# The weight and work tiles of an encoder kernel move to the top end of each SBUF partition

## The chip, the cores and the metric

The program runs on one core of one Trainium2 chip. The metric is the device time of one execution in microseconds (us); the matmul engine is called PE here, VectorE DVE, ScalarE ACT, GpSimd POOL. Before the change the median of three runs is 1266.83 us.

## The reference

A bidirectional encoder of four layers on 256 tokens with 1024 features, all in float32. Each layer is a token mixer and then a gated feed-forward block, both behind an RMS norm and with a residual add. The mixers are a gated short convolution (layers 0 and 3), attention in a neighbourhood (layer 1) and a Hyena long convolution (layer 2).

```python
for i in range(DEPTH):
    h = rmsnorm(x, norm_mix_g[i])
    y = short_conv_mixer(...) | neighborhood_attention(...) | hyena_mixer(...)
    x = x + y
    x = x + swiglu(rmsnorm(x, norm_ffn_g[i]), f_w13[i], f_w2[i])   # (silu(g) * u) @ w2, 2816 wide
```

## The kernel before, in words

Every weight passes through once. `wload` (lines 97 to 113) fetches a piece of 128 x 1024 floats by DMA into a tile `st`, has ACT round it into `hi` (float32r, line 107), and has DVE or POOL put the rest, `st - hi`, into `lo` (line 110). `st` has 5 buffers, `hi` and `lo` 6 each; all of them have 4096 bytes in a partition. Activations are split in the same way, so each product is three matmuls: high by high, low by high, high by low.

There are two kinds of matmul. In one the activations are the stationary operand (128 columns) and the weights stream past as the moving operand, 512 columns wide: `matmul3`, lines 127 to 131. It serves the first feed-forward product (tiles `pg`; 4 layers x 528 = 2112 matmuls, stationary tiles `xs`), the second (`accw`; 4 x 264 = 1056, stationary tiles `hid`), and the out-projections of the mixers (`accao`, `accbo`, `accco`; 192, 96 and 96, stationary tiles `mid`). In the other the weights are stationary and 256 columns of activations move: `mm3`, lines 115 to 120, for the in-projections of the short convolutions (`ai`, 1152) and of the Hyena mixer (`ci`, 576). The attention's in-projection (`bi`, 576, lines 549 to 551) has stationary activations and 256 moving columns of weights. Some small products of the long convolution's filters use the same forms (`ff`, `fh`).

The order of the work is the order in which the code is written, with small tables of lags (lines 41 to 50) for what is put between the matmuls; the change touches none of it. Between the pieces of the first feed-forward product stand four transposes each (`pth`, line 329), and in layers 0 and 1 the filters' small products.

SBUF tiles come from pools. A pool takes its room when it is opened, next to the pool opened before it, and gives it back when it is closed. Five pools stay open all the time (lines 58 to 62): `const`, `xsp` (tiles `xs`), `wst` (`st`), `wsp` (`hi`, `lo`) and `tp` (work tiles). The pools of a stage, such as those with `hid`, `mid` and the filters' tiles, are opened on top of them and closed with the stage.

Of the kernel before, what the change touches and what calls it, by code (L numbers as in the profile page):

```python
# [53 lines left out]
def encoder(ctx: ExitStack, tc: tile.TileContext, A: dict, out: bass.AP):  # L54
    nc = tc.nc
    ve, ac, pe, gp, sy = nc.vector, nc.scalar, nc.tensor, nc.gpsimd, nc.sync

    const = ctx.enter_context(tc.tile_pool(name="const", bufs=1))
    xsp = ctx.enter_context(tc.tile_pool(name="xsp", bufs=8))
    wst = ctx.enter_context(tc.tile_pool(name="wst", bufs=5))  # L60
    wsp = ctx.enter_context(tc.tile_pool(name="wsp", bufs=6))
    tp = ctx.enter_context(tc.tile_pool(name="tp", bufs=8))
    pp = ctx.enter_context(tc.tile_pool(name="pp", bufs=8, space=PSUM))
    dram = ctx.enter_context(tc.tile_pool(name="dram", bufs=1, space=DRAM))

# [922 lines left out]
```

## Time and profile before

| | us |
|---|---|
| median of 3 runs (1265.57 to 1267.26) | 1266.83 |
| the profiled execution's own time | 1265.59 |
| its span in the profile | 1263.7 |
| PE busy | 1217.6 (96%) |
| PE weight loads busy, beside the matmuls | 1055.2 (84%) |
| DVE busy | 841.5 (67%) |
| ACT busy | 636.2 (50%) |
| POOL busy | 272.9 (22%) |

[...] The rate is read from the starts: the time between the first and the last start of an unbroken row of matmuls, by the number of steps. The mean granted clock of PE is 0.99 of full speed, and the DMA queues move 182 GB/s on average.

### The profile page before, as it was taken

Reading aid. Unit: us, or ns where it says so; the run is one execution under the profiler, and the core shown is the slowest. Engines: PE = TensorE matmul, PEld = TensorE weight load, DVE = VectorE, ACT = ScalarE, POOL = GpSimd, SP = SyncE. Lnnn points to the kernel's source line nnn. Section 1 sums busy time; section 2 is a strip of 40 time slices with the busy share of each in tenths; the row PEclk is TensorE's granted clock in tenths of the full one; section 3 lists DMA queues with packets and bytes.
Section 4 is the critical chain, followed back from the end, with each engine's and each line's share of the span. In section 5 each row is a group of like instructions: output and inputs, shape, how many; then the busy total and the mean of one; then the engine's idle time right before and its main releaser. Section 6 shows DMA issues by size and latency. Waiting matters only on the chain.

```text
span 1263.7 us, 17703 instructions
## 1 busy us (share of the span) xinstructions
PE 1217.6 (96%) x6748; PEld 1055.2 (84%) x6748; DVE 841.5 (67%) x1023; ACT 636.2 (50%) x963; POOL 272.9 (22%) x228
## 2 busy tenths in 40 slices
PE   7999999999998999999988888999999999999998
PEld 7997888788998888887878887888888998888887
DVE  6867676786676647757678997655554776655542
ACT  6545554445576655543464444644443554544431
POOL 0111122333354212223226775000000000000000
PEclk9999999999999999999999999999999999999999
DMA  8656656565665565675754434556654655656661
GB/s 312 218 182 228 180 179 196 156 221 186 193 193 180 150 191 176 197 215 165 225 184 123 128 102 149 184 183 185 188 190 153 205 184 162 204 184 185 185 191 52
DMA packets 66892, 229.51 MB, mean 182 GB/s; under 512 B 9654, under 2 KB 10040, under 8 KB 66552
## 3 DMA queue, kind: packets, MB, share of 16 engines
q1 hardware_dynamic: 59824, 212.73, 53.9%
q0 software_dynamic: 4656, 9.73, 2.6%
q10 hardware_dynamic: 2328, 5.93, 1.4%
q8 instruction: 53, 0.87, 0.3%
q14 instruction: 31, 0.25, 0.1%
HBM read 222.04 MB, written 6.29 MB: 181 GB/s over the span
## 4 chain that ended last, share of the span: by engine, by line
PE 84%; DVE 9%; issue 2%; POOL 2%; ACT 2%; DMA 2%; ACTq 0%; SPq 0%; DVEq 0%; POOLq 0%
PE pg L129 13%; PE pg L131 13%; PE pg L130 13%; PE accw L129 6%; PE accw L131 6%; PE accw L130 6%; PE pth L329 2%; PE ai1a L118 1%; PE ai0a L119 1%; PE ai1a L119 1%; PE ai1a L120 1%; DMA bm<-in_rpb 1%; PE ai0a L120 1%; PE ai0a L118 1%; PE accao L131 1%
## 5 line engine op out<-in xcount | busy, mean ns | idle before, releaser
L76 DVE TENSOR_TENSOR low<-stw,hiw 128x1024 fp32r<-128x1024 f32 x246 | 304.8, 1243 | 225.9 <-ACT hiw L107 224.3
L107 ACT CAST hiw<-stw 128x1024 fp32r<-128x1024 f32 x268 | 280.7, 1052 | 298.6 <-PE pg L130 142.2
L129 PE MATMUL pg<-hiw,xsf 128*128 128x512 f32 x704 | 278.5, 397 | 0.5 <-ACT xsf L146 0.5
L131 PE MATMUL pg<-low,xsf 128*128 128x512 f32 x704 | 275.0, 391 | 0.0
L130 PE MATMUL pg<-hiw,xsf 128*128 128x512 f32 x704 | 274.3, 390 | 0.0
L131 PEld LDWEIGHTS pg<-low,xsf 128*128 128x128 f32 x704 | 132.4, 188 | 28.5
L129 PEld LDWEIGHTS pg<-hiw,xsf 128*128 128x128 f32 x704 | 132.4, 188 | 28.3 <-ACT xsf L146 1.9
L130 PEld LDWEIGHTS pg<-hiw,xsf 128*128 128x128 f32 x704 | 132.7, 188 | 26.6 <-DVE xsf L147 0.2
L129 PE MATMUL accw<-hiw,hid 128*128 128x512 f32 x352 | 139.7, 397 | 0.0
L131 PE MATMUL accw<-low,hid 128*128 128x512 f32 x352 | 138.5, 393 | 0.0
L130 PE MATMUL accw<-hiw,hid 128*128 128x512 f32 x352 | 138.0, 392 | 0.0
L76 POOL TENSOR_TENSOR low<-stw,hiw 128x1024 fp32r<-128x1024 f32 x22 | 54.4, 2474 | 171.4 <-ACT hiw L107 157.0
L131 PEld LDWEIGHTS accw<-low,hid 128*128 128x128 f32 x352 | 66.0, 188 | 15.9
L130 PEld LDWEIGHTS accw<-hiw,hid 128*128 128x128 f32 x352 | 66.2, 188 | 14.6
L129 PEld LDWEIGHTS accw<-hiw,hid 128*128 128x128 f32 x352 | 66.3, 188 | 14.0
L107 ACT CAST hiai<-stai 128x1024 fp32r<-128x1024 f32 (+1 forms) x49 | 48.8, 1013 | 38.4 <-PE ai1a L119 8.1
L76 DVE TENSOR_TENSOR loai<-stai,hiai 128x1024 fp32r<-128x1024 f32 (+1 forms) x49 | 56.9, 1178 | 15.7 <-ACT hiai L107 15.4
L320 ACT ACTIVATE sg<-pg,rtf 128x256 f32<-128x256 f32 x88 | 41.0, 468 | 45.2 <-PE pg L131 45.0
L321 DVE SCALAR_TENSOR_TENSOR hh<-pg,rtf,sg 128x256 f32<-128x256 f32 x88 | 41.8, 480 | 26.0 <-ACT sg L320 25.9
L118 PE MATMUL ci<-xsm,hici 128*128 128x256 f32 x192 | 56.6, 297 | 0.0
L551 PE MATMUL bi<-lobi,xsm 128*128 128x256 f32 x192 | 54.3, 283 | 2.0 <-DVE lobi L76 2.0
L550 PE MATMUL bi<-hibi,xsm 128*128 128x256 f32 x192 | 54.3, 283 | 1.7 <-DVE xsm L147 1.7
(243 smaller groups left out, 2478.0 us busy)
## 6 DMA issues: line engine op xcount, KB each, us to landing
stw<-in_f_w SPq DMA_DIRECT2D x264, 512.0 KB, 3.7
stai<-in_a_w_in SPq DMA_DIRECT2D x45, 512.0 KB, 4.3
stbi<-in_b_w_qkv SPq DMA_DIRECT2D x24, 512.0 KB, 4.2
stci<-in_c_w_in SPq DMA_DIRECT2D x24, 512.0 KB, 3.9
stao<-in_a_w_out SPq DMA_DIRECT2D x16, 512.0 KB, 3.7
hf<-ht POOLq DMA_DIRECT2D x16, 256.0 KB, 3.6
stbo<-in_b_w_out SPq DMA_DIRECT2D x8, 512.0 KB, 4.5
hq<-hf ACTq DMA_DIRECT2D x8, 512.0 KB, 3.6
```

The costliest lines, as they stand in the source:

```text
L76: (eng or ve).tensor_tensor(out=out_, in0=a, in1=b, op=op)
L107: ac.copy(out=hi[:, c], in_=st[:, c])
L118: pe.matmul(ps, hi[:, ws], xh, start=first, stop=False, **kw)
L119: pe.matmul(ps, hi[:, ws], xl, start=False, stop=False, **kw)
L120: pe.matmul(ps, lo[:, ws], xh, start=False, stop=last, **kw)
L129: pe.matmul(ps, xh, hi, start=first, stop=False, skip_group_check=True)
L130: pe.matmul(ps, xl, hi, start=False, stop=False, skip_group_check=True)
L131: pe.matmul(ps, xh, lo, start=False, stop=last, skip_group_check=True)
L320: ac.activation(sg, ps[h][:, :T], AF.Silu, scale=r)
L321: ve.scalar_tensor_tensor(out=hh[:, h * T : (h + 1) * T], in0=ps[h][:, T:], scalar=r, in1=sg, op0=ALU.mult, op1=ALU.mult)
L550: pe.matmul(o_, xl, hi[:, c], start=False, stop=False, skip_group_check=True)
L551: pe.matmul(o_, xh, lo[:, c], start=False, stop=k == KT - 1, skip_group_check=True)
```

## The change

Four of the five lasting pools are opened with `side="right"`: their tiles are packed from the top end of the partition down, and the pools of the stages, with `xsp`, from the bottom end up.

```diff
-    const = ctx.enter_context(tc.tile_pool(name="const", bufs=1))
+
+    wsp = ctx.enter_context(tc.tile_pool(name="wsp", bufs=6, side="right"))
+    wst = ctx.enter_context(tc.tile_pool(name="wst", bufs=5, side="right"))
+    tp = ctx.enter_context(tc.tile_pool(name="tp", bufs=8, side="right"))
+    const = ctx.enter_context(tc.tile_pool(name="const", bufs=1, side="right"))
     xsp = ctx.enter_context(tc.tile_pool(name="xsp", bufs=8))
-    wst = ctx.enter_context(tc.tile_pool(name="wst", bufs=5))
-    wsp = ctx.enter_context(tc.tile_pool(name="wsp", bufs=6))
-    tp = ctx.enter_context(tc.tile_pool(name="tp", bufs=8))
```

Both programs have the same instructions on every engine, in the same order and with the same waits; source lines from 58 on have a number higher by one. What differs are addresses. The table gives the first byte of each group of tiles in its partition, and that byte's remainder by 1024. All tiles of a group are whole multiples of 1024 bytes apart, and the operands inside them begin at steps of 512 bytes, so the remainder by 512 is that of every operand of the group.

| tiles | first byte before | remainder | first byte after | remainder |
|---|---|---|---|---|
| `xs` | 26624 | 0 | 16512 | 128 |
| `st` | 43008 | 0 | 159712 | 992 |
| `hi` | 63488 | 0 | 180192 | 992 |
| `lo` | 88064 | 0 | 204768 | 992 |
| `hid`, layers 0 and 1 | 176864 | 736 | 70304 | 672 |
| `hid`, layers 2 and 3; `mid` of A and C; `x` of the first norm | 139456 | 192 | 32896 | 128 |
| `mid` of B | 166752 | 864 | 60192 | 800 |
| filters' `dfth`, `pm`, `hd`; attention's `mask` | 150240 | 736 | 43680 | 672 |
| attention's `bm` | 187360 | 992 | 80800 | 928 |

(For a group of several pools the first byte is that of the tile named first.) The layers' `hid` differ because in layers 0 and 1 the filters' tiles lie below them.

## Rows read from the trace of the kernel before

**Rows 1.** The page's chain that ended last: shares by engine, then by line.
```profile
PE 84%; DVE 9%; issue 2%; POOL 2%; ACT 2%; DMA 2%; ACTq 0%; SPq 0%; DVEq 0%; POOLq 0%
PE pg L129 13%; PE pg L131 13%; PE pg L130 13%; PE accw L129 6%; PE accw L131 6%; PE accw L130 6%; PE pth L329 2%; PE ai1a L118 1%; PE ai0a L119 1%; PE ai1a L119 1%; PE ai1a L120 1%; DMA bm<-in_rpb 1%; PE ai0a L120 1%; PE ai0a L118 1%; PE accao L131 1%
```
**Rows 2.** The page's costliest groups: busy us, mean ns, idle time before and its releaser.
```profile
L107 ACT CAST hiw<-stw 128x1024 fp32r<-128x1024 f32 x268 | 280.7, 1052 | 298.6 <-PE pg L130 142.2
L129 PE MATMUL pg<-hiw,xsf 128*128 128x512 f32 x704 | 278.5, 397 | 0.5 <-ACT xsf L146 0.5
...
L129 PE MATMUL accw<-hiw,hid 128*128 128x512 f32 x352 | 139.7, 397 | 0.0
```
**Rows 3.** Timeline of PE, first feed-forward product, layer 2: start us, duration us, what.
```profile
802.31 0.39 PE L129 MATMUL pg<-hiw,xsf 128*128 128x512 f32 x1
...
805.03 0.39 PE L129 MATMUL pg<-hiw,xsf 128*128 128x512 f32 x1
```
**Rows 4.** Timeline of PE, first feed-forward product, layer 1, after the four transposes.
```profile
485.47 0.60 PE L329 MATMUL pth<-ident,hh 128*128 128x128 f32 x4
...
486.14 0.40 PE L130 MATMUL pg<-hiw,xsf 128*128 128x512 f32 x1
...
488.23 0.39 PE L130 MATMUL pg<-hiw,xsf 128*128 128x512 f32 x1
```
**Rows 5.** Timeline of PE, second feed-forward product, layer 1: first and last of a row.
```profile
607.91 0.40 PE L129 MATMUL accw<-hiw,hid 128*128 128x512 f32 x1
...
630.09 0.39 PE L131 MATMUL accw<-low,hid 128*128 128x512 f32 x1
```
**Rows 6.** Timeline of PE, second feed-forward product, layer 2: first and last of a row.
```profile
923.87 0.40 PE L130 MATMUL accw<-hiw,hid 128*128 128x512 f32 x1
...
972.86 0.39 PE L131 MATMUL accw<-low,hid 128*128 128x512 f32 x1
```
**Rows 7.** Both stretches by window, `accw` alone: busy (count), granted clock, DMA share, GB/s.
```profile
607.90:630.10 22.20, 22.18 (x96) 1.00 0.84 268
923.87:972.87 49.00, 49.00 (x216) 1.00 0.61 193
```
**Rows 8.** Timeline of PE, in-projection of layer 3, and the window's count of matmuls.
```profile
998.22 0.29 PE L119 MATMUL ai1a<-xsm,hiai 128*128 128x256 f32 x1
...
1049.82 0.28 PE L120 MATMUL ai1b<-xsm,loai 128*128 128x256 f32 x1
...
998.21:1049.82 51.61, 51.61 (x432) 1.00 0.62 193
```
**Rows 9.** Timeline of PE, a filter's product in layer 0 and the matmul after it.
```profile
192.44 0.28 PE L120 MATMUL fh<-pm,dfth 128*128 128x256 f32 x1
...
192.92 0.39 PE L129 MATMUL pg<-hiw,xsf 128*128 128x512 f32 x1
```
**Rows 10.** Timeline of PE, another filter's product in layer 0 and the matmul after it.
```profile
167.72 0.28 PE L657 MATMUL ff<-low,hd 128*128 128x256 f32 x1
...
168.54 0.40 PE L129 MATMUL pg<-hiw,xsf 128*128 128x512 f32 x1
```
**Rows 11.** Tile `hid` on DVE, layer 0, then layers 2 and 3: ns min/median/max.
```profile
L76 DVE TENSOR_TENSOR hid<-pth,hid x11: 627/684/692, 122.3 to 245.5; 128x512 fp32r<-128x512 f32 x11
...
L76 DVE TENSOR_TENSOR hid<-pth,hid x22: 682/685/686, 811.6 to 1206.4; 128x512 fp32r<-128x512 f32 x22
```
**Rows 12.** DMA issues by tile: queue, count, KB each, us to landing.
```profile
bm<-in_rpb SPq DMA_DIRECT2D x8, 256.0 KB, 4.4
...
x<-in_x ACTq DMA_DIRECT2D x1, 256.0 KB, 4.3
...
mask<-in_mask ACTq DMA_DIRECT2D x1, 256.0 KB, 3.8
```

## The prediction

> **What bounds the kernel now.** I begin with the chain that ended last: PE holds 84% of it, the first feed-forward product `pg` 3 x 13%, the second, `accw`, 3 x 6% [rows 1]. The groups say the same from the other side: before a `pg` matmul PE sat idle for 0.5 us in all, while ACT, which prepares the weights, stood waiting 142.2 us for PE [rows 2]. So in these stretches every nanosecond by which one matmul starts later than the last is paid in full, and the views to read are those of the pace: the start of the first and of the last of an unbroken row of matmuls.
>
> [...]
> - `pg`, settled: 12 steps in 2.72 us, 226.7 ns [rows 3]. For about ten matmuls after each four transposes it is slower: 9 steps in 2.09 us, 232.2 ns [rows 4]. With 38 settled and 10 of these among 48 the mean is 227.8 ns (an estimate).
> - `accw` in layer 1: 95 steps in 22.18 us, 233.5 ns [rows 5, 7].
> - `accw` in layer 2: 49.0 us for 214 steps (the window's 216 count one that was already running), 228.9 ns [rows 6, 7].
>
> Code, shapes and counts of the two `accw` stretches are one, and no other matmul stands between them. What I find different is where the stationary tile begins. In layer 1 it begins at 736, an odd multiple of 32 bytes, and the moving one at 0; in layer 2 at 192, a multiple of 64; in `pg` at 0 (all by the table of first bytes). This orders the three paces: 0 is best, 192 costs 1.1 to 2.2 ns more, 736 costs 4.6 more than 192. So PE's pace in this kernel depends on addresses, and addresses are all that the change touches.
>
> For 256 moving columns the settled pace is 120.0 ns with both operands at 0: 430 steps in 51.60 us [rows 8]. A filter's product whose two operands both begin at 736 also runs at 120 ns: 4 steps in 0.48 us [rows 9]. That speaks for the distance between the two remainders as what counts, not for each one alone. Another, with 0 against 736, runs 7 steps in 0.82 us, 117.1 ns [rows 10], but it is a burst of eight and never settles.
>
> **The change, part by part.** No instruction, wait or order changes, so there is nothing to cost but addresses.
>
> *ACT, DVE, POOL.* Nothing. The split into `hid` takes DVE 684 ns where the tile begins at 736 and 685 where it begins at 192 [rows 11]. ACT had to wait for PE anyway, so even a small loss would lie behind PE.
>
> *DMA.* Nothing. 256 KB land in 3.8 us in `mask` (736) and 4.4 in `bm` (992), in 4.3 in `x` (192) [rows 12]; in the steady stretch the queues are busy 0.61 of the time [rows 7], so weights that came a third slower would still be hidden.
>
> *PE, 512 columns.* All weights now begin at 992. Against the stationary tiles the distance becomes
> - `pg`: 128 against 992, 160 (an odd multiple of 32). No row has a moving tile at an odd multiple of 32 with 512 columns. The ends are the paces of the rows, 226.7 and 233.5; the nearest row in distance is layer 1's `accw`, so I take 233.5. That is 5.7 ns on 2112 matmuls: +12.0 us.
> - `accw` in layers 2 and 3, `accao` and `accco`, 528 + 192 + 96 = 816: also 160. From 228.9 to 233.5, +4.6 ns: +3.8 us.
> - `accw` in layers 0 and 1 and `accbo`, 528 + 96 = 624: 672 against 992, 704; 800 against 992, 832. Both are multiples of 64, as in layer 2 now. From 233.5 to 228.9: -2.9 us.
>
> *PE, 256 columns.* `ai`, `ci` and `bi`, 1152 + 576 + 576 = 2304 matmuls, get the distance 160 too. The lower end is 117.1 ns [rows 10], -2.9 ns each, -6.7 us; the upper end is the same 6.5 to 6.8 ns that 512 columns lose, 15 us. I take 0, since the settled 120 holds at 0 and at 736 alike, and keep both ends.
>
> The sum is 12.0 + 3.8 - 2.9 = **+12.9 us**, all on the chain, since nothing else limits these stretches. On the profiled execution's 1265.6 that is 1278.5; the median of the runs stands 1.2 above it, so I forecast **1279.7 us**. With the ends of the 256-column term the case reaches from 1273 to 1295.
>
> [...] Rows 5 and 6 show a pace that goes with the place of the stationary tile, 233.5 against 228.9 ns. [...]
>
> **The rivals.**
> - *Each operand counts by itself, the moving one too.* Then `pg` and the 816 lose as above, +15.8 us, and the 624 gain nothing, or lose another 6.5 ns each (4.1 us): +15.8 to +19.9, 1282.6 to 1286.7 us. Against it: rows 9, where both operands are at 736 and nothing is lost.
> - *Only the stationary operand counts.* The faster side. `xs`, `hid` of layers 2 and 3 and `mid` of A and C now begin at 128, a step of 128 as 0 is and 192 isn't, so `pg` stays and the 816 go from 228.9 to 226.7: -1.8 us. `ai` and `ci` (1728) get stationary weights at 992 and may run as in rows 10, -2.9 ns: -5.0 us. Together 0 to -6.8 us, 1260 to 1266.8, most likely 1263. It is decided in the in-projections: over 0.2% if more than about a third of them run at 117 ns. For it: rows 5 and 6 vary the stationary place alone. Against it: rows 9 show no difference from rows 8 though the stationary tile is at 736.
> - *Addresses don't matter at all;* layer 1's `accw` is slow for another reason, such as what the rest of the chip's engines do beside it (the DMA share is 0.84 there and 0.61 in layer 2 [rows 7]). 1266.8 us. Against it: 95 and 214 steps at one steady pace each, through changing work beside them.
> - *The two ends of the partition don't disturb each other.* Two operands far apart might be read without loss. From 226.7 for 512 columns and 120.0 for 256, a column takes 0.417 ns, and about 13 ns of each matmul are not columns. All of it saved on 3552 + 2304 matmuls is 76 us; a part of it would do for 1240. Against it: before the change layer 2's `hid` lies at 139456 and up and the weights at 63488 to 112640, in different halves already, and its pace is no better than that of `pg`.
>
> **How the numbers follow.** About 0.2% (2.5 us) is what a measurement of this kernel can tell from no change. My case has a chance of 0.40; each operand by itself 0.17; only the stationary 0.25, of which 0.17 fall over 0.2% faster and 0.08 within; no matter 0.13; far ends 0.05. So slower 0.40 + 0.17 = 0.57, the same 0.08 + 0.13 = 0.21, faster 0.17 + 0.05 = 0.22. The range, 1261 to 1288, takes in the rivals from the stationary one's middle to the upper end of the first; outside it lie the far ends, a tail of the stationary case, and the part of my case in which 256 columns lose more than half of their upper end. As cases of both signs hold most of the chance: my case alone has 1273 to 1288 as its range.
>
> **What would show it.** In the profile after: settled `pg` at about 233 ns where it is 226.7 now, `accw` in layer 2 at 233 and in layer 1 at 229, so that the two change places; `ai` still at 120; DVE, ACT and DMA durations unchanged. If `accw` of layer 1 stays at 233 while `pg` loses, each operand counts by itself; if `pg` stays at 227, only the stationary one does. The prediction is wrong if `pg` keeps its pace, or if the paces of rows 5 and 6 stay as they are.

## The result and the profile after

The changed kernel takes 1276.24 us (median of four runs, 1273.81 to 1277.22), the kernel before 1267.05 in the same comparison: a ratio of 1.0072, 95% interval 1.0054 to 1.0089, so +9.2 us. The forecast was 1279.7, range 1261 to 1288, slower with 0.57.

The page of the changed kernel first: the chain that ended last and the costliest groups. Line numbers are higher by one than before.

```profile
PE 81%; DVE 9%; POOL 3%; DMA 2%; issue 2%; ACT 1%; SPq 0%; ACTq 0%; DVEq 0%; POOLq 0%
PE pg L130 13%; PE pg L131 13%; PE pg L132 13%; PE accw L130 6%; PE accw L131 6%; PE accw L132 6%; DMA bm<-in_rpb 2%; PE pth L330 2%; POOL hrt L77 1%; PE ai1a L119 1%; DVE U L77 1%; PE ai0a L120 1%; PE ai1a L120 1%; PE ai1a L121 1%; DVE a L77 1%
...
L108 ACT CAST hiw<-stw 128x1024 fp32r<-128x1024 f32 x268 | 280.2, 1051 | 306.3 <-PE pg L131 144.0
L130 PE MATMUL pg<-hiw,xsf 128*128 128x512 f32 x704 | 282.3, 402 | 0.5 <-ACT xsf L147 0.5
```

They look as before [rows 1, 2]: PE holds the chain, `pg` waits for nothing, ACT takes as long and waits for PE. Only durations hint at where 10.2 us of span (1263.7 to 1273.9) went: the first `pg` line has a mean of 402 ns in place of 397, and PE is busy for 1228.3 us in place of 1217.6. The starts of matmuls show it. Timeline of PE in the changed kernel, start and duration in us, two matmuls of each unbroken row and, in brackets, the steps between them: `pg` in layer 2 (36 steps), `accw` in layer 1 (84), `accw` in layer 2 (204), `ai` in layer 3 (420).

```profile
838.79 0.39 PE L131 MATMUL pg<-hiw,xsf 128*128 128x512 f32 x1
...
847.19 0.39 PE L131 MATMUL pg<-hiw,xsf 128*128 128x512 f32 x1
...
612.57 0.40 PE L131 MATMUL accw<-hiw,hid 128*128 128x512 f32 x1
...
632.17 0.40 PE L131 MATMUL accw<-hiw,hid 128*128 128x512 f32 x1
...
931.86 0.39 PE L131 MATMUL accw<-hiw,hid 128*128 128x512 f32 x1
...
979.46 0.39 PE L131 MATMUL accw<-hiw,hid 128*128 128x512 f32 x1
...
1005.84 0.28 PE L120 MATMUL ai1a<-xsm,hiai 128*128 128x256 f32 x1
...
1055.68 0.28 PE L120 MATMUL ai1b<-xsm,hiai 128*128 128x256 f32 x1
```

And two windows of the same trace (length, PE busy and count, granted clock, DMA share, GB/s), `accw` alone in the first and all of PE in the second, for the counts:

```profile
929.77:979.69 49.92, 49.92 (x215) 1.00 0.63 189
...
1004.77:1055.79 51.02, 51.02 (x432) 1.00 0.65 199
```

So, in ns from start to start: `pg` 8.40 / 36 = 233.3 (226.7 before [rows 3]); `accw` of layer 2 47.60 / 204 = 233.3 (228.9 [rows 6]); `accw` of layer 1 19.60 / 84 = 233.3 in this row (233.5 [rows 5]); `ai` of layer 3 49.84 / 420 = 118.7 (120.0 [rows 8]), all at a granted clock of 1.00.

`accw` of layers 0 and 1 has two paces now. In layer 0 (36 steps, then 24) it runs at 8.24 / 36 = 228.9 and 5.60 / 24 = 233.3:

```profile
278.81 0.39 PE L131 MATMUL accw<-hiw,hid 128*128 128x512 f32 x1
...
287.05 0.39 PE L131 MATMUL accw<-hiw,hid 128*128 128x512 f32 x1
...
294.31 0.40 PE L131 MATMUL accw<-hiw,hid 128*128 128x512 f32 x1
...
299.91 0.40 PE L131 MATMUL accw<-hiw,hid 128*128 128x512 f32 x1
```

Measured from one stage's first matmul to the next stage's, the 10.2 us are made up like this:

| stage | after less before, us | forecast, us |
|---|---|---|
| `pg`, four layers | 1.04 + 2.93 + 2.75 + 2.78 = +9.5 | +12.0 |
| `accw` of layers 2 and 3, `accao` twice, `accco` | 1.11 + 1.15 + 0.41 + 0.40 + 0.39 = +3.5 | +3.8 |
| `accw` of layers 0 and 1, `accbo` | -0.76 - 0.24 - 0.03 = -1.0 | -2.9 |
| in-projections: `ai` twice, `bi`, `ci` | -1.25 - 0.93 + 0.01 + 0.41 = -1.8 | 0 (-6.7 to +15) |
| sum | +10.2 | +12.9 |

Layer 0's `pg` stands out with 1.04. That is the clock of the execution before, not the change: in its last quarter, after PE had waited 2.01 us for `hh`, the granted clock was 0.50 from 231.49 to 232.77 us, and there three steps of `pg` take 1.28 us, 427 ns each. These rows and the window of the kernel before, then the changed kernel's window:

```profile
229.64 1.20 PE L329 MATMUL pth<-ident,hh 128*128 128x128 f32 x4 [2.01 <-DVE hh L321]
...
231.49 0.63 PE L131 MATMUL pg<-low,xsf 128*128 128x512 f32 x1
...
232.77 0.63 PE L131 MATMUL pg<-low,xsf 128*128 128x512 f32 x1
...
204.00:237.00 33.00, 30.99 (x139) 0.95 0.62 180
...
204.00:238.00 34.00, 32.25 (x149) 1.00 0.63 184
```

At 0.95 in place of 1.00, 5% of 33 us is 1.7 us (an estimate), and with it layer 0 would show 2.7 like the others. In the first experiment below, which has the paces of before, this stage took 1.6 us less than in the execution before.

### The profile page after: what moved, and what is told of

It reads as the page before. It is cut to its first block, busy times and chain, and to the rows that moved or that the text cites. A ratio compares the mean times of both kernels' runs of the same rounds, so it can differ in the third digit from the quotient of the medians.

```text
span 1273.9 us, 17703 instructions
## 1 busy us (share of the span) xinstructions
PE 1228.3 (96%) x6748; PEld 1053.0 (83%) x6748; DVE 840.1 (66%) x1023; ACT 635.9 (50%) x963; POOL 272.4 (21%) x228
## 4 chain that ended last, share of the span: by engine, by line
PE 81%; DVE 9%; POOL 3%; DMA 2%; issue 2%; ACT 1%; SPq 0%; ACTq 0%; DVEq 0%; POOLq 0%
PE pg L130 13%; PE pg L131 13%; PE pg L132 13%; PE accw L130 6%; PE accw L131 6%; PE accw L132 6%; DMA bm<-in_rpb 2%; PE pth L330 2%; POOL hrt L77 1%; PE ai1a L119 1%; DVE U L77 1%; PE ai0a L120 1%; PE ai1a L120 1%; PE ai1a L121 1%; DVE a L77 1%
## 5 line engine op out<-in xcount | busy, mean ns | idle before, releaser
L77 DVE TENSOR_TENSOR low<-stw,hiw 128x1024 fp32r<-128x1024 f32 x246 | 305.2, 1245 | 233.1 <-ACT hiw L108 232.4
L108 ACT CAST hiw<-stw 128x1024 fp32r<-128x1024 f32 x268 | 280.2, 1051 | 306.3 <-PE pg L131 144.0
L130 PE MATMUL pg<-hiw,xsf 128*128 128x512 f32 x704 | 282.3, 402 | 0.5 <-ACT xsf L147 0.5
L131 PE MATMUL pg<-hiw,xsf 128*128 128x512 f32 x704 | 277.2, 394 | 0.0
```

The lines of the kernel that those rows point to most:

```text
L77: (eng or ve).tensor_tensor(out=out_, in0=a, in1=b, op=op)
L108: ac.copy(out=hi[:, c], in_=st[:, c])
L130: pe.matmul(ps, xh, hi, start=first, stop=False, skip_group_check=True)
L131: pe.matmul(ps, xl, hi, start=False, stop=False, skip_group_check=True)
```

## The experiments

The theory of the forecast: PE's pace depends on the **distance**, the stationary operand's first byte less the moving one's. Its rivals: each operand's own start counts; only the stationary one's does; or the **ends**, how far apart in the partition the operands lie. "Before" is 1266.2 to 1266.3 us in the comparisons below.

**All tiles 32 bytes higher.**

```diff
     const = ctx.enter_context(tc.tile_pool(name="const", bufs=1))
+    const.tile([P, 8], F32, name="pad")
```

> The kernel before, with 32 bytes put under all tiles, so that every tile begins 32 bytes higher: weights at 32, xs at 32, hid at 768 and 224, all distances as before. Distance theory: settled pg 226.7 ns, accw of layer 1 233.5, of layer 2 228.9, ai 120.0; time that of the kernel before, 1267. Each operand by itself: pg, which now has two operands at odd multiples of 32, at 233 or more, accw of layer 1 (now with a stationary tile at a multiple of 64) lower; about +12 us, 1279. Only the place in the partition (ends): no change, 1267.

1266.46 us, ratio 1.0002 (0.9993 to 1.0012). `pg` of layer 2, 36 steps in 8.16 us:

```profile
833.38 0.39 PE L131 MATMUL pg<-hiw,xsf 128*128 128x512 f32 x1
...
841.54 0.39 PE L131 MATMUL pg<-hiw,xsf 128*128 128x512 f32 x1
```

That is 226.7 ns with both operands at 32, and `accw` keeps 233.3 and 228.9. Each operand by itself, which wanted +12 us, falls.

**The weights 32 bytes higher, nothing at another end.**

```diff
     xsp = ctx.enter_context(tc.tile_pool(name="xsp", bufs=8))
+    ctx.enter_context(tc.tile_pool(name="pad", bufs=1)).tile([P, 8], F32, name="pad")
     wst = ctx.enter_context(tc.tile_pool(name="wst", bufs=5))
```

> The kernel before, with 32 bytes between xs and the weights, so that weights, work tiles, hid and mid begin 32 bytes higher and xs stays; nothing goes to another end. Distance theory: pg (distance 480, an odd multiple of 32) at 233.3 ns, accw as before (233.5 and 228.9, the distances are kept), ai and ci (distance 32) near 118; +11.6 for pg, -3.4 for the in-projections, about +8 us, 1275. Each operand by itself: accw of layer 2, with both operands moved by 32, at 233 or more too, 1278. Ends theory: nothing, 1267.

1273.12 us, ratio 1.0051 (1.0034 to 1.0068): +6.9. `pg` of layer 2 (36 steps), `accw` of layer 2 (204), `ai` of layer 3 (420):

```profile
840.87 0.40 PE L131 MATMUL pg<-hiw,xsf 128*128 128x512 f32 x1
...
849.27 0.40 PE L131 MATMUL pg<-hiw,xsf 128*128 128x512 f32 x1
...
933.87 0.39 PE L131 MATMUL accw<-hiw,hid 128*128 128x512 f32 x1
...
980.56 0.39 PE L131 MATMUL accw<-hiw,hid 128*128 128x512 f32 x1
...
1006.98 0.28 PE L120 MATMUL ai1a<-xsm,hiai 128*128 128x256 f32 x1
...
1056.68 0.28 PE L120 MATMUL ai1b<-xsm,hiai 128*128 128x256 f32 x1
```

8.40 / 36 = 233.3, 46.69 / 204 = 228.9, 49.70 / 420 = 118.3: close to the +8 expected. `pg` loses although its stationary tiles stay where they were, which ends "only the stationary operand"; `accw` of layer 2, both of whose operands moved, loses nothing. One pad of 32 bytes makes most of the whole change's loss.

**At the two ends, with the remainders of before.**

```diff
+    padr = ctx.enter_context(tc.tile_pool(name="padr", bufs=1, side="right")).tile([P, 248], F32, name="padr")
     wsp = ctx.enter_context(tc.tile_pool(name="wsp", bufs=6, side="right"))
...
+    padl = ctx.enter_context(tc.tile_pool(name="padl", bufs=1)).tile([P, 224], F32, name="padl")
     xsp = ctx.enter_context(tc.tile_pool(name="xsp", bufs=8))
+    padm = ctx.enter_context(tc.tile_pool(name="padm", bufs=1)).tile([P, 48], F32, name="padm")
```

> The changed kernel, weights and work tiles at the top end, with three unused tiles that give every tile the remainder by 1024 that it had before the change. Distance theory: all paces as before, pg 226.7 ns, accw 233.5 and 228.9, ai 120.0, time 1267. Each operand by itself: the same, 1267. Ends theory (that operands lie far apart is what costs): it stays at 1276.

1265.05 us, ratio 0.9993 (0.9984 to 1.0003). The tiles lie at the ends as in the changed kernel, and the whole loss is gone; `pg` of layer 2, 36 steps in 8.15 us:

```profile
835.86 0.39 PE L134 MATMUL pg<-hiw,xsf 128*128 128x512 f32 x1
...
844.01 0.39 PE L134 MATMUL pg<-hiw,xsf 128*128 128x512 f32 x1
```

So it is the remainders and not the ends, in either direction: lying far apart costs nothing and gains nothing that can be measured.

**Which distances.** Three kernels give `xs` another start in each layer, by a wider buffer and an offset:

```diff
-            xs = xsp.tile([P, 2, T], F32R, tag="xs", name=f"xs{self.name}_{m}")
+            o_ = XS_AT[self.name] // 4
+            xs = xsp.tile([P, 2 * T + 128], F32R, tag="xs", name=f"xs{self.name}_{m}")
+            xs = xs[:, o_ : o_ + 2 * T].rearrange("p (j t) -> p j t", j=2)
```

> The kernel before, with the xs tiles begun 32, 96, 16 and 8 bytes into their buffers in the feed-forward blocks of layers 0 to 3, and 32, 32, 96 and 16 bytes in the mixers; weights, hid and mid stay. Distance theory: pg at 233 ns in layers 0 and 1 (odd multiples of 32); for 16 and 8 in layers 2 and 3 no row exists, between 226.7 and 236 by the ends of the rows; ai of layer 0 and ci near 118; accw as before in all layers. If only whole steps of 32 count, layers 2 and 3 stay at 226.7. Ends theory: nothing moves.

> The kernel before, with xs begun 64, 128, 256 and 448 bytes into its buffers in the feed-forward blocks of layers 0 to 3 (64, 128, 128, 256 in the mixers); all else stays. Distance theory with steps of 64: pg at 226.7 to 228.9 ns in all four, none at 233. If the step is 128: 226.7 at 128 and 256, 228.9 at 64 and 448. If it is finer than that or no step at all counts: values up to 234 among them.

> The kernel before, with xs begun 4, 24, 40 and 504 bytes into its buffers in the feed-forward blocks of layers 0 to 3 (8, 16, 48, 4 in the mixers); all else stays. By the one row there is (230.7 ns at 8 bytes): 4 bytes between 226.7 and 230.7, 24 and 40 at 233 as 16 and 32 have it, 504 (8 below the next 512) like 8, near 230.7. If a smaller distance than 64 always costs all, 233 in all four.

One execution each, 1272.64, 1269.64 and 1276.30 us; only their paces are used. The settled pace of `pg`, each from 36 steps in the trace, by the distance in bytes; below it stand the pairs of rows for 256 and 448, and a row of 30 steps at 16:

| distance | 4 | 8 | 16 | 24 | 32 | 40 | 64 | 96 | 128 | 256 | 448 | 504 |
|---|---|---|---|---|---|---|---|---|---|---|---|---|
| ns | 232.4 | 230.7 | 233.3 | 231.1 | 233.3 | 233.3 | 233.3 | 234.4 | 232.6 | 226.7 | 228.9 | 233.3 |

```profile
838.20 0.39 PE L131 MATMUL pg<-hiw,xsf 128*128 128x512 f32 x1
...
846.36 0.39 PE L131 MATMUL pg<-hiw,xsf 128*128 128x512 f32 x1
...
1119.45 0.39 PE L131 MATMUL pg<-hiw,xsf 128*128 128x512 f32 x1
...
1127.69 0.39 PE L131 MATMUL pg<-hiw,xsf 128*128 128x512 f32 x1
...
806.18 0.39 PE L130 MATMUL pg<-hiw,xsf 128*128 128x512 f32 x1
...
812.98 0.40 PE L132 MATMUL pg<-low,xsf 128*128 128x512 f32 x1
```

My class "multiples of 64" is not one. Of the distances tried only 0 and 256 have 226.7 in every settled row; 448 has 228.9 as 192 has [rows 6], and these two are the same by 256; all else, 64 and 128 among them, is between 230.7 and 234.4 in the table. Of the four values of the last kernel only 40 came as expected: 4 and 504 cost more, 24 less. Nor does a distance always have one pace: at 16 the layer's first row settles at 226.7 (6.80 us for 30 steps, the last pair) and all later ones at 233.3; at 24 rows have 231.1 or 230.0. With 256 moving columns 0 and 256 are not the best: `ai` settles at 120.0 there, at 116.7 with the moving tile 32 bytes ahead, and at 123.3 with 4. `ci` with 96, expected near 118, stayed at 120.0.

**One half of the stationary tiles off.**

```diff
+XS_AT = {'f1': (264, False), 'f2': (264, True), 'f3': (272, False)}
...
+            w_, back = XS_AT.get(self.name, (T, False))
+            xs = xsp.tile([P, 2 * T + 128], F32R, tag="xs", name=f"xs{self.name}_{m}")
+            xs = xs[:, : 2 * w_].rearrange("p (j t) -> p j t", j=2)[:, :, :T]
+            xs = xs[:, ::-1] if back else xs
```

> The kernel before, with only one half of each stationary tile moved in the feed-forward blocks: in layer 1 the low halves of xs at 32 and the high ones at 0, in layer 2 the high halves at 32 and the low ones at 0, in layer 3 the low halves at 64; layer 0 as before. In each three matmuls of layer 1 one stationary tile is off, in layer 2 two are. If a matmul is slowed while a stationary tile at an off distance is loaded for the next one: in layer 1 one start in three is late, the one after the first of the three (line 131 here or its neighbour), mean 226.7 + 6.7 / 3 = 228.9 ns; in layer 2 two in three, mean 231.1. If one off tile is enough to spoil the whole row's rhythm: 233.3 in both. Layer 3 between 226.7 and 228.9.

One execution, 1270.66 us. `pg`, 36 steps each, settles at 226.7 in layer 0 and at 233.3, 232.2 and 231.1 in layers 1 to 3; layers 1 and 2:

```profile
475.55 0.39 PE L131 MATMUL pg<-hiw,xsf 128*128 128x512 f32 x1
...
483.95 0.39 PE L131 MATMUL pg<-hiw,xsf 128*128 128x512 f32 x1
...
836.69 0.40 PE L131 MATMUL pg<-hiw,xsf 128*128 128x512 f32 x1
...
845.05 0.40 PE L131 MATMUL pg<-hiw,xsf 128*128 128x512 f32 x1
```

One tile of three off by 32 costs as much as all three, and two of three cost less than one; neither expectation for layer 2, nor that for layer 3, came. So the loss isn't a sum over the matmuls concerned. In layer 1 the step up to line 131, whose stationary tile is the one that is off, is the longest, 239 ns, but the other two are 228 and 233 and not 226.7 (means of 12), and with all three tiles off, in the changed kernel, the same step is the longest too (237). Whether a matmul is slowed while the next one's stationary tile is loaded, this run doesn't tell.

**The changed kernel with 96 bytes at the top.**

```diff
+    ctx.enter_context(tc.tile_pool(name="pad", bufs=1, side="right")).tile([P, 24], F32, name="pad")
     wsp = ctx.enter_context(tc.tile_pool(name="wsp", bufs=6, side="right"))
```

> The changed kernel with 96 unused bytes at the very top, so that the weights begin at remainder 896 in place of 992; nothing goes to another end, and the activations stay. The distance of pg, of accw in layers 2 and 3, of accao, accco and of the in-projections becomes a multiple of 256 (768 by 1024), that of accw in layers 0 and 1 an odd multiple of 32. Distance theory, counted by 256: pg settled at 226.7, accw of layers 2 and 3 at 226.7 (228.9 before the change, -2.2 on 816 matmuls, -1.8 us), accw of layers 0 and 1 at 233.3 and ai, ci at 120.0 as before the change: about 1265, 2 us under the kernel before, 11 under the changed one. Counted by 1024: pg at a pace of its own, not 226.7, time between 1266 and 1276. Ends theory: 1276, as the changed kernel.

1265.03 us, ratio 0.9988 (0.9979 to 0.9997). `pg` of layer 2 (36 steps), `accw` of layer 2 (204), `accw` of layer 1 (84):

```profile
833.71 0.39 PE L132 MATMUL pg<-hiw,xsf 128*128 128x512 f32 x1
...
841.87 0.39 PE L132 MATMUL pg<-hiw,xsf 128*128 128x512 f32 x1
...
924.62 0.39 PE L132 MATMUL accw<-hiw,hid 128*128 128x512 f32 x1
...
970.86 0.39 PE L132 MATMUL accw<-hiw,hid 128*128 128x512 f32 x1
...
608.57 0.40 PE L132 MATMUL accw<-hiw,hid 128*128 128x512 f32 x1
...
628.17 0.40 PE L132 MATMUL accw<-hiw,hid 128*128 128x512 f32 x1
```

8.16 / 36 = 226.7 at the distance 256 (128 less 896; the expectation's 768 takes the operands the other way round), 46.24 / 204 = 226.7, 19.60 / 84 = 233.3: all as expected, and the time to a microsecond. As the stationary tiles of one buffer lie 512 bytes apart, these rows hold 768 as well as 256, and those of before 512 as well as 0: the best distances count by 256. And 24 unused floats turn the change's +9.2 us into -1.2.

**All distances chosen.** The kernel before with unused bytes ahead of `hid` and `mid`, and `xs` of the mixers of layers 0, 2 and 3 begun 32 bytes into its buffers.

```diff
+XS_AT = {'f0': 0, 'f1': 0, 'f2': 0, 'f3': 0, 'm0': 32, 'm1': 0, 'm2': 32, 'm3': 32}
...
     tp = ctx.enter_context(tc.tile_pool(name="tp", bufs=8))
+    ctx.enter_context(tc.tile_pool(name="pad", bufs=1)).tile([P, 208], F32, name="pad")
...
-        with tc.tile_pool(name=f"ffn{layer}", bufs=NP_) as hp:
+        with tc.tile_pool(name=f"pad{layer}", bufs=1) as pd, tc.tile_pool(name=f"ffn{layer}", bufs=NP_) as hp:
+            pd.tile([P, 120 if layer < 2 else 256], F32, name=f"pad{layer}")
...
+            cp.tile([P, 88], F32, name="padb")
             mids = new_mids(cp, "B")
```

> The kernel before, with unused bytes ahead of hid and mid so that they begin at remainder 0 like the weights, and with xs of the mixers in layers 0, 2 and 3 begun 32 bytes into its buffers, so that the in-projections have the distance 480. Distance theory: pg settled at 226.7 as before, accw 226.7 in all layers (from 233.3 in layers 0 and 1, -6.7 on 528, -3.5 us; from 228.9 in 2 and 3, with accao and accco -2.2 on 816, -1.8 us), ai and ci at 116.7 (-3.3 on 1728, -5.7 us): about -11 us, 1255. Each operand by itself: accw as well, the in-projections not foreseen. Ends theory: no change, 1266.

1259.12 us, ratio 0.9935 (0.9917 to 0.9952): -7.2 us, faster than both kernels, though not by the -11 expected. `accw` of layer 1 (84 steps) and layer 2 (204), `ai` of layer 3 (420):

```profile
607.50 0.39 PE L132 MATMUL accw<-hiw,hid 128*128 128x512 f32 x1
...
626.54 0.39 PE L132 MATMUL accw<-hiw,hid 128*128 128x512 f32 x1
...
923.37 0.39 PE L132 MATMUL accw<-hiw,hid 128*128 128x512 f32 x1
...
969.61 0.39 PE L132 MATMUL accw<-hiw,hid 128*128 128x512 f32 x1
...
995.87 0.28 PE L121 MATMUL ai1a<-xsm,hiai 128*128 128x256 f32 x1
...
1044.87 0.28 PE L121 MATMUL ai1b<-xsm,hiai 128*128 128x256 f32 x1
```

The settled paces came as expected, 19.04 / 84 = 226.7, 46.24 / 204 = 226.7, 49.00 / 420 = 116.7. Part of what is missing is the clock. In the profiled execution (1260.10 us) the granted clock was lower for a while in layer 1's in-projection, after PE had waited 2.06 us for `lobi` (0.80 over the 17 us below), and this stage took 2.2 us longer than before:

```profile
303.00:320.00 17.00, 13.94 (x94) 0.80 0.69 235
```

Of the six executions the two with a mean granted clock of 0.989, the median of the kernel before, took 1254.45 and 1255.48 us, as expected; the four with 0.986 and 0.987 took 1258.94 to 1262.27. Whether this kernel brings the lower clock about stays open. Another part is `ci`: its stage took 132.8 us although its matmuls came at 117, and 132.7 in the kernel with the old remainders at the two ends, where they came at 120, with a granted clock of 0.91 in both. There PE waits some 20 us for DVE and POOL either way (20.7 us in the kernel before, 20.1 in the changed one). In layer 0 `ai` settled at 117.8 and not at 116.7. And `accw` of layers 0 and 1 gained 1.6 and 1.0 us where 1.8 each was expected, probably since the matmuls after each interruption are slower, as in rows 4 (232.2 ns for `pg`).

## Why the prediction was right, and where it was not

*What bounds the kernel: right.* The stages in which PE sets the pace took the whole loss, and ACT, DVE and DMA kept their durations: ACT's `hiw` 1052 and 1051 ns, DVE's `hid` of layers 2 and 3 685 [rows 11] and 683, and the DMA share in the steady stretch 0.61 [rows 7] and 0.63.

*The pace depends on where the stationary tile begins relative to the moving one: right,* and shown by moving both (no change), one (+6.9 us), and by putting the old remainders at the new ends (no change). With 32 bytes between `xs` and the weights `pg` went from 226.7 to 233.3 ns. What in PE makes it so isn't shown.

*`pg`, +12.0: right.* +9.5 between the stages, +11.2 with the lower clock of the execution before put aside. *The 816, +3.8: right,* +3.5. But 233.5 for the distance 160 was in part luck. Its reason, the odd multiple of 32, is no class, and of the distances with a row 192 is nearer to 160 than 736 is; its 228.9 would have made `pg` +2.3. It came out because nearly every distance other than 0 and 256 costs `pg` 4 to 8 ns.

*The 624, -2.9: this step failed.* I put distances into two classes, odd and even multiples of 32, on the strength of one value each (736, and 192). They count by 256: `accbo`'s 832 is 64 by that, and at 64 `pg` too has 233.3, so it gained nothing. 704 is 192 by 256 and can have 228.9, but `accw` in layers 0 and 1 fell into 228.9 in some rows and 233.3 in others. Together -1.0.

*256 columns, 0 with ends of -6.7 and +15: the value taken was wrong, the lower end was on the right side.* I took the burst of [rows 10] for unsettled; the in-projections at 480, which by 256 is the same as its 736, settle at 116.7 (in one stage of three at 117.8). Nor is 160 the distance of `ai` and `ci`: their weights are the stationary operand, so it is 992 less 128, 864; only `bi` has 160. `ai` gained 1.25 and 0.93 us. `ci` came at 117 to 118 ns as well and gained nothing, for there PE waits anyway (20.1 us), which I had not asked.

The two misses, +1.9 and -1.8, cancel in the sum, which is luck. What is left between +12.9 and +10.2 is the clock of the execution before (1.7), the rest of `pg` (0.8, as its mean step grew by 5.2 to 5.5 ns and not by 5.7) and of the 816 (0.3); the medians differ by 9.2.

*The rivals.* Each operand by itself would have been 1282.6 or more: no. Only the stationary: no. (That it needed a third of the in-projections at 117 ns to be over 0.2% faster is a slip: with its -1.8 us of the 816, a seventh would have done.) No matter: no; and the DMA share doesn't make layer 1's `accw` slow, for with all distances chosen it runs at 226.7 with 0.83. Far ends: no, lying apart changes nothing.

## What to carry to other kernels

A pool's side, a new constant or a pad of 32 bytes moves every tile opened after it, and in a stretch that PE bounds that was worth 0.5% to 0.7% here with not one instruction of the work changed. Read the pace of unbroken matmul rows from their starts, form by form, and if equal forms differ, compare the first bytes of both operands before looking for a wait. Then choose the distance by trial: here a multiple of 256 for 512 moving columns, and 32 bytes for 256.

## What the runs showed of the hardware that was not expected

The pace is not one value for a distance. At 704 one and the same loop ran for several rows at 228.9 and for others at 233.3 ns, each repeating to a nanosecond, and at 16 for one row at 226.7 and then at 233.3. How a row is entered may matter as well; no run tried it. What within PE makes the pace depend on the distance stays open: that one stationary tile off out of three (233.3 ns) costs more than two (232.2) speaks against a fixed price per load, and no run took the loads away.
